# An MLP in two stages of seven-product recursion: source order on four engines, single passes from twelve to twenty

## The chip, the cores and the metric

The kernel runs on one core of one Trainium2 chip. Times are device microseconds (us) of one execution; the time of a kernel is the median of several executions. PE is the matrix engine (TensorE), DVE the vector engine, ACT the scalar engine, POOL the GpSimd engine, and SP the engine from whose queue all transfers of this kernel's MLP are issued. PSUM is the memory that PE writes products to.

## The reference

One layer of an encoder, applied to 1024 and to 256 tokens (1280 in all, width 1024): a mixing stage with DeltaNet and attention heads, and then the MLP, which is all that this change touches.

```
x = x + rmsnorm(mix, norm_mix_post)
hm = rmsnorm(x, norm_mlp_pre)
f = square(relu(hm @ w_up)) @ w_down          # w_up: 1024 x 4096, w_down: 4096 x 1024, float32
y = x + rmsnorm(f, norm_mlp_post)
```

## The kernel before, in words

*Precision.* A float32 product is made of three fast products: each operand is split into a high part, made by a cast on ACT, and a low part, made by a subtraction on DVE or POOL (`split`, lines L79 and L80). PE then adds hi times hi, hi times lo and lo times hi.

*Recursion.* Both matrix products of the MLP are computed blockwise by a scheme that makes a product of 2 x 2 blocks from seven products instead of eight. For the up product the 2 x 2 blocks are of `w_up` (256 columns of it, one "pair", two blocks of 512 rows by two of 128 columns) and of the normalised tokens. The scheme needs four sums of weight blocks per pair (`up_sums`, tiles `us`, L1128 to L1131) and sums of token blocks, which `to_M` makes (L1039 to L1042). `prep_m(j, i)` splits token operand j of half i into `mh` and `ml`, 128 by 1280 each.

*Up stage.* The 1280 tokens form two halves. `PASSES` lists what is done: NF pairs with the first half alone ("single passes"), then the other pairs with both halves ("double passes"), then the first NF pairs with the second half alone. With NF = 6 that is 6 + 10 + 6 passes; there are 16 pairs. A pass has seven products (`UP`), and a product is 12 matmuls of 128 by 128 by 320 for each half (`up_mm`, L1145 to L1147). `up_w` makes the weights of one product ready: the cast on ACT (tile `uhi`) and the subtraction on DVE (tile `ulo`). `up_post` takes a product out of PSUM: product 0 by a copy on ACT (L1168), the others by an addition on DVE (L1171 to L1198, two for product 4); products 1, 4, 5 and 6 complete a block, which ACT passes through relu and square (L1154, L1155), and from products 5 and 6 POOL makes sums for the down stage (L1190 to L1192, L1201). SP stores the results to `r_d`.

*Order.* A planner, which has its own estimate of each instruction's time, puts every engine's instructions in order before the kernel runs; on the chip each engine then keeps to that list. The order of the source enters as a priority. In the loop over products `s`, weights are made two products ahead (`up_w(*seq[s + 2])`), in three places for `uhi` and three for `ulo`. The four sums of a pair stand together where its first weights are made, on DVE in single passes and on POOL in double ones. The second half's seven `prep_m` come every fourth product from s = 10. The last token tile's norm (`norm`) takes steps at s = 3 to 6, and `to_M` of the last three tiles comes at the start, at s = 1 and at s = 7.

*Down stage.* It reads the stored blocks back in 49 steps of seven products (`DN`), five row tiles each (`prod`, L1283 to L1285), and adds them into ten tiles `acc` in DVE (L1289, L1291). `down_load` loads and sums blocks of `w_down` on POOL (L1237 to L1242), `down_r` loads a row operand `fr`, `down_prep` splits both (L1265 to L1271). The first of these are placed inside the last single passes, at products counted by `k`. At the end the products of the first two pairs, done as plain blocks, go into `acc` tile by tile (L1452 to L1456), followed by `rest`: a multiplication with the norm's weights (L1422), the root of the mean square (L1425 to L1430), the final multiply-and-add (L1434) and the store.

Of the kernel before, what the change touches and what calls it, by code (L numbers as in the profile page):

```python
# [10 lines left out]
F32R = mybir.dt.float32r  # L11
# [3 lines left out]
ALU = mybir.AluOpType  # L15
# [46 lines left out]
def build(ctx, tc, I, O):  # L62
# [14 lines left out]
    def split(hi, lo, src, heng=None, leng=None):  # L77

        (S.copy if heng is None else heng)(hi, src)  # L79
        (V if leng is None else leng).tensor_tensor(lo, src, f32(hi), ALU.subtract)  # L80
# [912 lines left out]
    def run(g):  # L993
        try:
            while True:
                next(g)
        except StopIteration as e:
            return e.value
# [25 lines left out]
    def to_M(xn, t, eng=G):  # L1024
        g = []
        for i in range(2):
            tp = tr_tile("xt")
            for k in range(4):
                T.transpose(tp[:, k * 128:(k + 1) * 128], xn[:, (i * 4 + k) * 128:(i * 4 + k + 1) * 128], ident)
            g.append(tp.rearrange("p (k c) -> p k c", k=4))  # L1030
        for i, cs, ts in halves(t):
            g0, g1 = (x[:, :, ts] for x in g)
            if i == 0:
                for j, x in ((0, g0), (1, g1)):
                    S.copy(mc[j, t // HT][:, :, cs], x)
            else:
                b11, b21, b22, t4, t1, t2, t3 = (mc[j, t // HT][:, :, cs] for j in range(7))
                S.copy(b22, g1)
                V.tensor_tensor(t1, g0, b11, ALU.subtract)  # L1039
                V.tensor_tensor(t3, b22, g0, ALU.subtract)  # L1040
                eng.tensor_tensor(t2, b22, t1, ALU.subtract)
                eng.tensor_tensor(t4, t2, b21, ALU.subtract)  # L1042
# [3 lines left out]
    def prep_m(j, i, leng=None):  # L1046
        mh[j, i] = p_tile5(h_slot[j, i], name="mh", dt=F32R)
        ml[j, i] = p_tile5(mspare[0], name="ml", dt=F32R)
        split(mh[j, i], ml[j, i], mc[j, i], leng=leng)
        mtag[j, i], mspare[0] = mspare[0], m_slot[j, i]  # L1050


    NF = 6
    PASSES = [*((p, (0,)) for p in range(NF)), *((p, (0, 1)) for p in range(NF, NP)), *((p, (1,)) for p in range(NF))]
    raws = {}

# [64 lines left out]
    ua = {}  # L1121

    def up_sums(n):
        a11, a12, a21, a22 = (raws[n][:, k:k + 4, f:f + 128] for f in (0, 128) for k in (0, 4))
        s = [uw.tile([128, 4, 128], F32, tag=f"us{x}", name="us", bufs=1) for x in range(4)]
        ua[n] = [a11, a12, a22, *s]
        eng = V if PASSES[n][1] != (0, 1) else G
        eng.tensor_tensor(s[0], a21, a22, ALU.add)  # L1128
        eng.tensor_tensor(s[1], s[0], a11, ALU.subtract)
        eng.tensor_tensor(s[2], a11, a21, ALU.subtract)  # L1130
        eng.tensor_tensor(s[3], a12, s[1], ALU.subtract)  # L1131

    def up_w(n, i):

        if n not in ua:
            up_sums(n)
        hi = uw.tile([128, 4, 128], F32R, tag="uhi", name="uhi", bufs=3)
        lo = uw.tile([128, 4, 128], F32R, tag="ulo", name="ulo", bufs=3)
        split(hi, lo, ua[n][UP[i][0]])
        return hi, lo  # L1140

    def up_mm(w, b, i):
# [106 lines left out]
    def down_r(s):  # L1249
        fr[s] = ring("fr", s, (Q, HW))  # L1250
        SP.dma_start(out=fr[s], in_=r_src(s // 7, s))
# [9 lines left out]
    def down_prep(s):  # L1261

        n, i = divmod(s, 7)
        fo[s] = hi, lo = ring("fhi", s, (Q, HW), F32R), ring("flo", s, (Q, HW), F32R)
        S.copy(hi, fr[s])  # L1265
        if i % 2:
            G.tensor_tensor(lo, fr[s], f32(hi), ALU.subtract)
        dw[s] = w_split(n, DN[i][1], ring("dhi", s, (Q, 512), F32R))
        yield
        if i % 2 == 0:  # L1270
            V.tensor_tensor(lo, fr[s], f32(hi), ALU.subtract)  # L1271
        del fr[s]
# [19 lines left out]
                seen_acc.add((t, d))  # L1292


    ws = {0: (w0[:, 0], w0[:, 1])}
    norm = out_norm(NT - 1, *prev)
    xlate = prev[2]
    to_M(*late[0], V)
    up_sums(0)
    ws[1] = up_w(*seq[1])  # L1300
    for s, (n, i) in enumerate(seq):
        p, parts = PASSES[n]
        if s == 1:
            to_M(*late[1], V)
        if s + 2 < len(seq):
            ws[s + 2] = up_w(*seq[s + 2])
        w = ws.pop(s)
        for h in parts:
            up_post(p, i, h, up_mm(w, UP[i][1], h))
        if i == 6 and n + 2 < len(PASSES):  # L1310
            up_raw(n + 2)
        if s == 0:
            for _, j in UP[NM:]:
                prep_m(j, 0)
        if 2 < s < 7:
            next(norm, None)
        elif s == 7:
            to_M(xlate, NT - 1, V)
            nstack.close()
            mr = ctx.enter_context(pool("mr"))  # L1320
            h_slot |= {(j, 1): place(mr, j) for j in range(7)}
        if s > 9 and (s - 10) % 4 == 0 and s < 38:
            j = UP[(s - 10) // 4][1]
            prep_m(j, 1)
        k = s - (len(seq) - 7 * NF)
        if k == 0:

            hm = [[(h_slot[j, h], mtag[j, h]) for _, j in UP] for h in range(2)]
            a, b = ([mspare[0]] + [x for y in hm[0] for x in y]), [x for y in hm[1] for x in y] + [w_slot]
            slots = {("w", 0): a[0:8], "fr": [a[8], a[9], b[0]], "fhi": [a[10], a[11], b[2]], "flo": [a[12], a[13], b[3]],  # L1330
                     "dhi": [a[14], b[1], b[4]], ("w", 1): b[5:13]}
            extra = b[13:15]
        if k in (4, 12, 18, 24):
            down_load(0, (4, 12, 18, 24).index(k))
        k -= 7 * NF - 21
        if k in (-3, 1, 15, 18):
            down_r((-3, 1, 15, 18).index(k))
        if k in (8, 13):
            run(down_prep((8, 13).index(k)))
    us.close()  # L1340
    ac = ctx.enter_context(pool("ac", side="right"))
    acc = [ac.tile([128, DM], F32, name=f"acc{t}") for t in range(NT)]
# [73 lines left out]
    def rest(c, h, ss):  # L1416

        t = c + h * HT
        last = (c, h) == (HT - 1, 1)
        r = ac.tile([128, 4], F32, tag="rsq", name="rsq", bufs=3)  # L1420
        for d in range(2):
            (V if last else G).tensor_tensor(half(t, d), half(t, d), wpf[:, d * 512:d * 512 + 512], ALU.mult)  # L1422
            if not last:
                yield
        V.tensor_tensor(r[:, 0:1], ss[:, 0:1], ss[:, 1:2], ALU.add)  # L1425
        S.activation(r[:, 1:2], r[:, 0:1], AF.Sqrt, scale=1.0 / DM, bias=eps)
        V.tensor_scalar(r[:, 2:3], r[:, 0:1], -0.5 / DM, -0.5 * EPS, ALU.mult, ALU.add)
        V.reciprocal(r[:, 1:2], r[:, 1:2])
        V.scalar_tensor_tensor(r[:, 3:4], r[:, 1:2], r[:, 2:3], r[:, 1:2], ALU.mult, ALU.mult)  # L1429
        V.scalar_tensor_tensor(r[:, 3:4], r[:, 3:4], 1.5, r[:, 1:2], ALU.add, ALU.mult)  # L1430
        yield
        for c0, n in ((0, 512), (512, 512)) if c == HT - 1 else ((0, DM),):
            cs = slice(c0, c0 + n)
            V.scalar_tensor_tensor(acc[t][:, cs], acc[t][:, cs], r[:, 3:4], x1s[c][:, h, cs], ALU.mult, ALU.add)  # L1434
            for ps_, t0, t1 in rows_of(c, h):
                SP.dma_start(out=y_out(t0, t1, cs), in_=acc[t][ps_, cs])
        if h and c + 2 < HT:
            x1s[c + 2] = x1_tiles(c + 2)
# [4 lines left out]
    for c in range(HT):  # L1443
        tk = slice(c * 128, c * 128 + 128)
        for h in range(2):
            ss = ac.tile([128, 2], F32, tag="ss", name="ss", bufs=3)
            for d in range(2):
                pm = p_tile()
                for m in range(2):
                    r, w = lrow[h, m], lwt[m, d]  # L1450
                    for k in range(Q):
                        T.matmul(pm, lhsT=r[0][:, k, tk], rhs=w[0][:, k], start=(m == k == 0), stop=False)  # L1452
                        T.matmul(pm, lhsT=r[0][:, k, tk], rhs=w[1][:, k], start=False, stop=False)
                        T.matmul(pm, lhsT=r[1][:, k, tk], rhs=w[0][:, k], start=False, stop=(m == k == 1))
                t = c + h * HT
                V.tensor_tensor(half(t, d), half(t, d), pm, ALU.add)  # L1456
                S.activation(junk, half(t, d), AF.Square, accum_out=ss[:, d:d + 1])  # L1457
                for _ in range(2):
                    if rests and next(rests[0], "end") == "end":
                        rests.pop(0)  # L1460
            rests.append(rest(c, h, ss))
            if h == 0 and c + 1 < HT:
                fix(c + 1)
# [31 lines left out]
```

## Time and profile before

| what | value |
|---|---|
| median of 3 runs | 1739.7 us (1735.0 to 1739.98) |
| the profiled execution's own time | 1741.06 us |
| its span, first to last instruction | 1739.3 us |
| PE busy | 1626.4 us, 94% |
| DVE busy | 1267.9 us, 73% |
| ACT busy | 854.6 us, 49% |
| POOL busy | 735.8 us, 42% |
| mean granted PE clock | 0.981 |
| up products | 905.6 to 1332.5 us of the span |
| down products | 1332.5 to 1727.8 us |

The profile's page gives busy time by engine and by group of instructions, with the idle time of the engine before each group and what ended it. A view by stretches gives the busy time of every engine between two moments, and the timeline lists instructions in order with the start, the duration, the line, the tile written and read, and in brackets the idle time before it and what ended that. An engine's busy share over the span hides stages with different limits, so the stretches are read stage by stage.

### The profile page before, as it was taken

What the parts mean: (1) busy time and instruction counts of PE and PEld (TensorE: products, weight loads), DVE (VectorE), ACT (ScalarE), POOL (GpSimd) and SP (SyncE); (2) the same over time, 40 slices, a digit from 0 to 9 for tenths busy, and PEclk for the clock granted to TensorE, in tenths of its full rate; (3) what the DMA queues carried; (4) which work ended last, traced back from release to release, by engine and by line L of the source; (5) the groups of instructions that cost most, each with busy time, mean ns of one, the idle gap of its engine ahead of it and who ended that gap; (6) DMA issues with size and microseconds to landing.
All of it is one profiled execution on the core that took longest, in us unless ns stands there. A gap on an engine that the chain in (4) does not pass through costs nothing. (4 is left out here: it accounts for less than half of the span.)

```text
span 1739.3 us, 27944 instructions
## 1 busy us (share of the span) xinstructions
PE 1626.4 (94%) x9799; PEld 1387.8 (80%) x9799; DVE 1267.9 (73%) x2549; ACT 854.6 (49%) x1937; POOL 735.8 (42%) x658
## 2 busy tenths in 40 slices
PE   6999898898997999889988999999989999999997
PEld 5777776777775888668878999999888888888885
DVE  7546798996744778885759954545787978888777
ACT  5236566554345767674446644544465333333422
POOL 3212231321113334440102555554636777788763
PEclk9999999999998999999999999999999999999999
DMA  6113334445447866244333543444556544444234
GB/s 208 70 42 109 97 108 129 137 133 154 133 143 231 273 203 194 79 161 166 104 127 127 178 147 125 151 135 134 187 193 220 154 140 146 132 143 142 86 115 155
DMA packets 208779, 252.68 MB, mean 145 GB/s; under 512 B 35073, under 2 KB 163391, under 8 KB 208639
## 3 DMA queue, kind: packets, MB, share of 16 engines
q1 hardware_dynamic: 208495, 250.77, 45.9%
q8 instruction: 77, 1.26, 0.3%
q14 instruction: 63, 0.52, 0.1%
q0 software_dynamic: 144, 0.13, 0.0%
HBM read 159.75 MB, written 91.10 MB: 144 GB/s over the span
## 5 line engine op out<-in xcount | busy, mean ns | idle before, releaser
L1146 PE MATMUL pd<-mh,ulo 128*128 128x320 f32 x892 | 279.6, 314 | 12.9 <-DVE ulo L80 12.8
L1145 PE MATMUL pd<-mh,uhi 128*128 128x320 f32 x892 | 276.6, 311 | 5.5 <-ACT uhi L79 5.5
L1147 PE MATMUL pd<-ml,uhi 128*128 128x320 f32 x892 | 276.9, 311 | 0.0
L1289 DVE TENSOR_TENSOR acc<-acc,pd 128x512 f32<-128x512 f32 x330 | 206.7, 678 | 44.1 <-PE pd L1285 44.1
L1283 PE MATMUL pd<-dhi,fhi 128*128 128x512 f32 x490 | 192.2, 392 | 1.0 <-DVE acc L1291 1.0
L1284 PE MATMUL pd<-dl,fhi 128*128 128x512 f32 x490 | 192.3, 393 | 0.0
L1285 PE MATMUL pd<-dhi,flo 128*128 128x512 f32 x490 | 191.9, 392 | 0.0
L1146 PEld LDWEIGHTS pd<-mh,ulo 128*128 128x128 f32 x892 | 169.1, 190 | 17.8 <-DVE ulo L80 17.8
L367 PE MATMUL pt<-h_hi,whi 128*128 128x512 f32 (+1 forms) x480 | 178.5, 372 | 0.0
L369 PE MATMUL pt<-h_hi,wlo 128*128 128x512 f32 (+1 forms) x480 | 178.4, 372 | 0.0
L368 PE MATMUL pt<-h_lo,whi 128*128 128x512 f32 (+1 forms) x480 | 178.4, 372 | 0.0
L1145 PEld LDWEIGHTS pd<-mh,uhi 128*128 128x128 f32 x892 | 168.9, 190 | 7.0 <-ACT uhi L79 7.0
L1147 PEld LDWEIGHTS pd<-ml,uhi 128*128 128x128 f32 x892 | 169.0, 190 | 0.0
L1265 ACT CAST fhi<-fr 128x1280 fp32r<-128x1280 f32 x49 | 62.1, 1267 | 212.6 <-PE pd L1284 116.2
L80 POOL TENSOR_TENSOR dl<-dw,dhi 128x1024 fp32r<-128x1024 f32 x49 | 129.0, 2633 | 43.4 <-ACT dhi L79 42.8
L1190 POOL TENSOR_TENSOR s<-u,u 128x320 f32<-128x320 f32 x32 | 34.3, 1071 | 207.6 <-ACT u L1155 140.7
L727 POOL TENSOR_TENSOR P<-P,sm 128x512 f32<-128x512 f32 (+1 forms) x72 | 73.5, 1040 | 95.3 <-DVE sm L725 39.0
L1283 PEld LDWEIGHTS pd<-dhi,fhi 128*128 128x128 f32 x490 | 92.0, 188 | 22.4 <-DVE acc L1291 1.4
L1285 PEld LDWEIGHTS pd<-dhi,flo 128*128 128x128 f32 x490 | 92.0, 188 | 20.7
L1284 PEld LDWEIGHTS pd<-dl,fhi 128*128 128x128 f32 x490 | 92.0, 188 | 20.3
L80 DVE TENSOR_TENSOR ulo<-us,uhi 128x512 fp32r<-128x512 f32 x88 | 76.3, 869 | 43.4 <-ACT uhi L79 42.5
L367 PEld LDWEIGHTS pt<-h_hi,whi 128*128 128x128 f32 x480 | 92.7, 193 | 13.5
(358 smaller groups left out, 4091.0 us busy)
## 6 DMA issues: line engine op xcount, KB each, us to landing
fr<-r_d SPq DMA_DIRECT2D x49, 640.0 KB, 4.3
vis<-vis_d SPq DMA_DIRECT2D x64, 384.0 KB, 4.2
uraw<-in_w_up SPq DMA_DIRECT2D x22, 1024.0 KB, 5.4
r_d<-s SPq DMA_DIRECT2D x128, 160.0 KB, 1.8
r_d<-u SPq DMA_DIRECT2D x96, 160.0 KB, 2.1
dw<-in_w_down SPq DMA_DIRECT2D x28, 512.0 KB, 4.9
wraw<-in_w_in SPq DMA_DIRECT2D x48, 256.0 KB, 3.7
x<-in_x_prompt SPq DMA_DIRECT2D x16, 512.0 KB, 3.4
```

Source lines behind the costliest of these rows:

```text
L80: (V if leng is None else leng).tensor_tensor(lo, src, f32(hi), ALU.subtract)
L367: T.matmul(pm[:, :n], lhsT=whi, rhs=h_hi[:, k, t0:t0 + n], start=(k == 0), stop=False)
L368: T.matmul(pm[:, :n], lhsT=whi, rhs=h_lo[:, k, t0:t0 + n], start=False, stop=False)
L369: T.matmul(pm[:, :n], lhsT=wlo, rhs=h_hi[:, k, t0:t0 + n], start=False, stop=(k == KD - 1))
L727: G.tensor_tensor(x[:, :kw], x[:, :kw], sm[:, 0:1].to_broadcast([128, kw]), ALU.mult)
L1145: T.matmul(pm, lhsT=w[0][:, k], rhs=mh[b, i][:, k], start=(k == 0), stop=False)
L1146: T.matmul(pm, lhsT=w[1][:, k], rhs=mh[b, i][:, k], start=False, stop=False)
L1147: T.matmul(pm, lhsT=w[0][:, k], rhs=ml[b, i][:, k], start=False, stop=(k == 3))
L1283: T.matmul(pm, lhsT=r[0][:, k, tk], rhs=w[0][:, k], start=(k == 0), stop=False)
L1284: T.matmul(pm, lhsT=r[0][:, k, tk], rhs=w[1][:, k], start=False, stop=False)
L1285: T.matmul(pm, lhsT=r[1][:, k, tk], rhs=w[0][:, k], start=False, stop=(k == Q - 1))
L1289: V.tensor_tensor(half(t, d), half(t, d), pm, ALU.add)
```

## The change

- From the start of the up products to the end, PE, DVE, ACT and POOL issue their instructions in the order in which the source emits them; the planner orders SP alone, as before.
- NF is 10: passes are 10 + 6 + 10.
- Weights are made three products ahead. High and low part lie in one tile, and there are four places for it: three of their own (`u1` to `u3`) and `w_slot`, which held the first product's weights.
- The four sums of a pair are no longer emitted together: two after the weights of its product 1, one after those of product 2, one after those of product 4.
- The second half's `prep_m` come one per pass, at s = 14, 21, ... 56. The norm's steps move to s = 4, 5, 7 and 8, the last `to_M` to s = 10.
- The down stage's first loads and splits are placed over the ten last single passes: `down_load` at k = 10, 30, 36, 42, `down_r` at 20, 24, 66, 67, `down_prep` at 60 and 65.
- In the tail the last tile's multiplication with the norm's weights follows each of its two additions at once, the other tile of the last pair is multiplied on DVE instead of POOL, and three steps of the tile before are emitted after each product instead of two.

```diff
-    NF = 6
+    NF = 10
...
         eng = V if PASSES[n][1] != (0, 1) else G
+        yield
         eng.tensor_tensor(s[0], a21, a22, ALU.add)
         eng.tensor_tensor(s[1], s[0], a11, ALU.subtract)
+        yield
         eng.tensor_tensor(s[2], a11, a21, ALU.subtract)
+        yield
         eng.tensor_tensor(s[3], a12, s[1], ALU.subtract)
...
-        if n not in ua:
-            up_sums(n)
-        hi = uw.tile([128, 4, 128], F32R, tag="uhi", name="uhi", bufs=3)
-        lo = uw.tile([128, 4, 128], F32R, tag="ulo", name="ulo", bufs=3)
+        if n not in sums:
+            sums[n] = up_sums(n)
+            next(sums[n])
+        x = (7 * n + i) % 4
+        hl = (uw.tile([128, 2, 4, 128], F32R, tag=f"u{x}", name="uhl", bufs=1) if x else
+              p_tile5(w_slot, (2, 4, 128), "uhl", F32R))
+        hi, lo = hl[:, 0], hl[:, 1]
         split(hi, lo, ua[n][UP[i][0]])
+        if i in (1, 2, 4):
+            next(sums[n], None)
...
+    ctx.enter_context(tc.manual_schedule(engines={getattr(mybir.EngineType, x) for x in ("PE", "DVE", "Activation", "Pool")}))
...
+    ws[1] = up_w(*seq[1])
     to_M(*late[0], V)
-    up_sums(0)
-    ws[1] = up_w(*seq[1])
+    M1 = dict(zip(range(14, 14 + 7 * 7, 7), UP))
     for s, (n, i) in enumerate(seq):
         p, parts = PASSES[n]
-        if s == 1:
+        if s == 2:
             to_M(*late[1], V)
-        if s + 2 < len(seq):
-            ws[s + 2] = up_w(*seq[s + 2])
+        for x in (2, 3) if s == 0 else (s + 3,):
+            if x < len(seq):
+                ws[x] = up_w(*seq[x])
         w = ws.pop(s)
         for h in parts:
             up_post(p, i, h, up_mm(w, UP[i][1], h))
...
-        if s > 9 and (s - 10) % 4 == 0 and s < 38:
-            j = UP[(s - 10) // 4][1]
-            prep_m(j, 1)
+        if s in M1:
+            prep_m(M1[s][1], 1)
...
-        for d in range(2):
-            (V if last else G).tensor_tensor(half(t, d), half(t, d), wpf[:, d * 512:d * 512 + 512], ALU.mult)
-            if not last:
-                yield
+        for d in () if last else range(2):
+            (V if c == HT - 1 else G).tensor_tensor(half(t, d), half(t, d), wpf[:, d * 512:d * 512 + 512], ALU.mult)
+            yield
...
-                for _ in range(2):
+                if (c, h) == (HT - 1, 1):
+                    V.tensor_tensor(half(t, d), half(t, d), wpf[:, d * 512:d * 512 + 512], ALU.mult)
+                for _ in range(2 if c < HT - 1 else 3):
```

More of the change, by code (lines that the diff above doesn't have):

```diff
@@ L1127, in up_sums @@
         eng = V if PASSES[n][1] != (0, 1) else G
+        yield
         eng.tensor_tensor(s[0], a21, a22, ALU.add)
         eng.tensor_tensor(s[1], s[0], a11, ALU.subtract)
+        yield
         eng.tensor_tensor(s[2], a11, a21, ALU.subtract)
+        yield
         eng.tensor_tensor(s[3], a12, s[1], ALU.subtract)
+    sums = {}
     def up_w(n, i):
-        if n not in ua:
-            up_sums(n)
-        hi = uw.tile([128, 4, 128], F32R, tag="uhi", name="uhi", bufs=3)
-        lo = uw.tile([128, 4, 128], F32R, tag="ulo", name="ulo", bufs=3)
+        if n not in sums:
[5 more added lines that the diff above has]
+        hi, lo = hl[:, 0], hl[:, 1]
         split(hi, lo, ua[n][UP[i][0]])
+        if i in (1, 2, 4):
+            next(sums[n], None)
         return hi, lo
@@ L1311, in build @@
             up_raw(n + 2)
-        if s == 0:
+        if s == 1:
             for _, j in UP[NM:]:
                 prep_m(j, 0)
-        if 2 < s < 7:
+        if s in (4, 5, 7, 8):
             next(norm, None)
-        elif s == 7:
+        elif s == 10:
             to_M(xlate, NT - 1, V)
@@ L1332, in build @@
             extra = b[13:15]
[L1333 to L1339, printed above, removed]
+        if k in (10, 30, 36, 42):
+            down_load(0, (10, 30, 36, 42).index(k))
+        if k in (20, 24, 66, 67):
+            down_r((20, 24, 66, 67).index(k))
+        if k in (60, 65):
+            run(down_prep((60, 65).index(k)))
     us.close()
```

## The prediction

> **What bounds the kernel now.** I read the page first: TensorE (PE) is busy 94% of the span, and its lines L1145 to L1147 are the first products of the MLP. The idle time in front of them is small on the page, so I went on to busy time by stretch.
>
> ```profile
> span 1739.3 us, 27944 instructions
> PE 1626.4 (94%) x9799; PEld 1387.8 (80%) x9799; DVE 1267.9 (73%) x2549; ACT 854.6 (49%) x1937; POOL 735.8 (42%) x658
> L1146 PE MATMUL pd<-mh,ulo 128*128 128x320 f32 x892 | 279.6, 314 | 12.9 <-DVE ulo L80 12.8
> ```
>
> In the next view the stretches run from the last VectorE (DVE) operation of one pass, L1198, to that of the next; columns are length, then busy us of PE, weight loads, DVE, ACT, POOL, then the granted clock. The last two rows are the up products as a whole and the down products.
>
> ```profile
> 905.60:945.50 39.90, 32.41 (x199) 29.67 (x198) 37.72 (x67) 27.13 (x50) 4.76 (x4) 0.96 0.40 132
> 945.50:959.70 14.20, 13.09 (x87) 12.41 (x86) 14.20 (x22) 9.54 (x20) 6.17 (x4) 1.00 0.51 166
> 974.10:986.60 12.50, 11.84 (x77) 11.32 (x78) 12.50 (x21) 6.81 (x15) 3.33 (x3) 1.00 0.47 153
> 1022.80:1047.40 24.60, 24.60 (x170) 24.60 (x170) 12.18 (x21) 12.24 (x25) 12.77 (x13) 1.00 0.42 137
> 1246.10:1266.80 20.70, 12.89 (x77) 11.40 (x76) 15.77 (x19) 9.79 (x19) 12.39 (x9) 0.93 0.62 208
> 1305.40:1318.00 12.60, 12.60 (x88) 12.60 (x87) 11.32 (x19) 7.67 (x17) 4.21 (x4) 1.00 0.56 183
> 905.60:1332.50 426.90, 406.46 (x2707) 399.46 (x2706) 294.26 (x459) 234.66 (x465) 206.03 (x173) 0.99 0.48 158
> 1332.50:1727.80 395.30, 394.25 (x1712) 320.83 (x1711) 314.32 (x451) 127.80 (x149) 292.42 (x126) 1.00 0.44 138
> ```
>
> A pass with both halves (168 matmuls) takes 24.6 us with PE never idle, 0.146 us a matmul; so a product of 12 matmuls is 1.76 us and a single pass 12.3 us at best. All 2688 up matmuls need 394 us; the stretch is 427, so some 30 us (with 3 us of transposes) are what better ordering could win. They lie in the first four passes and at 1246 to 1267. The down products have 1 us of idle. Single passes are tight elsewhere: DVE is busy 11.3 of 12.6 us.
>
> **The change, part by part.** *Order.* From the up products on, four engines issue in source order. Per product s the source says: cast the weights of s+3 to hi (ACT), subtract to lo (DVE), perhaps weight sums (DVE), multiply (PE), then the post step of s: a DVE add from PSUM and, in products 1, 4, 5 and 6 of a pass, relu and square on ACT. ACT thus has cast(s+4) behind the relu pair of s, which waits for DVE's add of s; DVE has split(s+4) before its add of s+1. That closes a ring: add, relu, square, cast, split, next add. Before, the order was another: at 1316.78 the add of product 5 is followed by a split whose cast had already run, then the add of product 6, and only then the split whose cast follows the relu pair.
>
> ```profile
> 1309.28 1.25 DVE L1130 TENSOR_TENSOR us<-uraw 128x512 f32<-128x512 f32 x1
> 1315.78 0.48 DVE L1182 TENSOR_TENSOR u<-u,pd 128x320 f32<-128x320 f32 x1
> 1316.17 0.68 DVE L80 TENSOR_TENSOR ulo<-uraw,uhi 128x512 fp32r<-128x512 f32 x1
> 1316.78 0.48 DVE L1186 TENSOR_TENSOR u<-u,pd 128x320 f32<-128x320 f32 x1
> 1317.41 0.69 DVE L80 TENSOR_TENSOR ulo<-uraw,uhi 128x512 fp32r<-128x512 f32 x1 [0.15 <-ACT uhi L79]
> 1318.02 0.48 DVE L1198 TENSOR_TENSOR u<-u,pd 128x320 f32<-128x320 f32 x1
> 1318.81 0.96 DVE L80 TENSOR_TENSOR ulo<-us,uhi 128x512 fp32r<-128x512 f32 x1 [0.31 <-ACT uhi L79]
> ...
> 1306.91 0.41 ACT L1168 COPY u<-pd 128x320 f32<-128x320 f32 x1
> 1307.21 0.62 ACT L79 CAST uhi<-us 128x512 fp32r<-128x512 f32 x1
> 1317.29 0.47 ACT L1154 ACTIVATE u<-u 128x320 f32<-128x320 f32 x1
> 1318.17 0.60 ACT L79 CAST uhi<-us 128x512 fp32r<-128x512 f32 x1
> ...
> 1318.34 0.88 POOL L1190 TENSOR_TENSOR s<-u,u 128x320 f32<-128x320 f32 x1 [8.36 <-ACT u L1155]
> ```
>
> From the add (1316.78) over relu (1317.29), square and cast (1318.17) to the split (1318.81) is 2.03 us; the split holds DVE 0.60 (1316.17 to 1316.78): 2.63 us to the next add, where PE takes 1.76. An add alone holds DVE 0.40 (1315.78 to 1316.17), a sum, of the split's form, 0.60. One single pass in source order, counted from the start of its add 1, with PE never in the way:
>
> - add 2 at 2.63 (one ring); adds 3 and 4, with no relu between, each after an add and a split: 3.63 and 4.63;
> - add 5 after a ring and two sums, 8.46; add 6 after a ring and one sum, 11.69;
> - then, product 0 having no add: relu pair 1.39, cast 0.60, PSUM copy 0.30 (1306.91 to 1307.21), cast 0.60, split 0.60, sum 0.60: the next pass's add 1 at 15.78.
>
> Of the 15.8 us DVE waits over 6, in turn with ACT. POOL's sums of products 5 and 6 come on top, since they and DVE hold each other up where both read SBUF: beside POOL's 1318.34 the split at 1318.81 took 0.96 instead of 0.69, the sum at 1309.28 took 1.25. Three or four such operations a pass make some 1.2 us. I take 17.0, between 15.8 (no blocking) and 18 (twice that), because these rows are the same operations in the same neighbourhood.
>
> No row shows this order run, so the ring is my step from the code and the rows. That a queue is not overtaken, this trace shows: a cast of the down stage waits 5.09 us for its DMA, the weight cast behind it waits too, and PE with it.
>
> ```profile
> 1261.13 1.26 ACT L1265 CAST fhi<-fr 128x1280 fp32r<-128x1280 f32 x1 [5.09 <-DMA fr<-r_d]
> 1262.30 0.61 ACT L79 CAST uhi<-uraw 128x512 fp32r<-128x512 f32 x1
> ...
> 1262.96 0.41 PE L1145 MATMUL pd<-mh,uhi 128*128 128x320 f32 x1 [2.11 <-ACT uhi L79]
> 1265.96 0.63 PE L1146 MATMUL pd<-mh,ulo 128*128 128x320 f32 x1 [2.59 <-DVE ulo L80]
> ```
>
> [...]
>
> *Three ahead, four places.* One product more of slack, 1.76 us once; a ring that is longer than PE's pace uses any fixed slack up in its first pass.
>
> *Ten pairs alone.* Single passes go from 12 to 20, double ones from 10 to 6. PE's work stays; 28 more casts and splits, sums of eight more passes on DVE, four more loads of 1 MB. The stretch at 1305.40 carries such loads and stores at 183 GB/s with PE never idle, so the loads stay hidden; at PE's pace the rest would too; behind the ring each single pass costs 17.0 − 12.3 = 4.7 us. Double passes give the ring 3.5 us per product and put the sums on POOL: 24.6 stays.
>
> *Token halves prepared one per pass.* Before, two in a pass cost 1.9 us (14.20), one 0.2 (12.50). In source order its cast stands on ACT before the weight cast of product 1, and its subtraction on DVE before that split:
>
> ```profile
> 944.77 1.26 ACT L79 CAST mh<-mc 128x1280 fp32r<-128x1280 f32 x1
> 971.44 1.48 DVE L80 TENSOR_TENSOR ml<-mc,mh 128x1280 fp32r<-128x1280 f32 x1
> ...
> 924.65 1.27 DVE L1009 SCALAR_TENSOR_TENSOR x<-mix,rsq,x 128x1024 f32<-128x1024 f32 x1
> 925.96 1.06 ACT L1011 ACTIVATE mix<-x 128x1024 f32<-128x1024 f32 x1 [0.18 <-DVE x L1009]
> ...
> 1231.60 2.39 POOL L1237 TENSOR_TENSOR dw<-dw 128x1024 f32<-128x1024 f32 x1 [7.88 <-DMA dw<-in_w_down]
> 1231.72 2.82 DVE L1131 TENSOR_TENSOR us<-uraw,us 128x512 f32<-128x512 f32 x1
> ```
>
> The first two rows are its cast and subtraction. In the walk the last step becomes 1.39 + 0.60 + 0.30 + 1.26 + 1.48 + 0.60 + 0.60 = 6.23 for 4.09 (the weight cast now runs beside the subtraction): +2.1, so passes 2 to 8 take 19.1.
>
> *First two passes.* Two walks up to the last add (17.0 + 12.8), plus the seventh half 2.1, two tiles of token sums 2.4 each, the norm of the last tile 3.9 (1.27 and 1.06 in series, the rest small): 40.6 after the first add at 905.6 + 3.5, so 949.7 where it was 945.5.
>
> *Down stage's preparation.* Its DMAs are moved 40 products ahead of their casts, so the 5.09 us wait goes, and 8 us of the 20.70 us pass with it. In exchange four POOL sums of 1024 block a split each (between 0 and the 2.1 us of the last row, 2.82 for 0.69; I take 1.8 a piece, 7 us), and two preparations put a cast of 1.26 and a shorter one each into ACT's queue ahead of a weight cast, with a long DVE or POOL subtraction behind: 4 to 5 us each, 9 us. SP's queue stays the scheduler's; the stores wait on data they waited on before.
>
> *Tail.* The last tile's adds stood behind the tile before:
>
> ```profile
> 1727.35 0.40 PE L1454 MATMUL pd<-lwt,lrow 128*128 128x512 f32 x1
> 1729.39 0.68 DVE L1456 TENSOR_TENSOR acc<-acc,pd 128x512 f32<-128x512 f32 x1
> 1730.92 0.69 DVE L1422 TENSOR_TENSOR acc<-acc,wpf 128x512 f32<-128x512 f32 x1 [0.19 <-ACT junk L1457]
> 1733.66 0.15 DVE L1425 TENSOR_TENSOR rsq<-ss 128x1 f32<-128x1 f32 x1
> 1734.83 0.75 DVE L1434 SCALAR_TENSOR_TENSOR acc<-acc,rsq,x 128x512 f32<-128x512 f32 x1
> ```
>
> The last matmul ends at 1727.75, and 12 matmuls of 0.23 earlier the first of the tile's two products did, 1725.0, but its add came at 1729.39. Now it comes at 1725.0; multiply at 1726.5 (the 1.53 of the rows), the other tile's two multiplies and root chain (1.17) to 1729.5; second add, multiply to 1731.6; two final steps 1.4, root chain, to 1734.2 instead of 1734.83: −0.6 (−2 to +1). The down loop keeps its order in kind: 0 ± 3, less its 1 us of idle.
>
> *Sum.* Last add of pass 1 949.7; passes 2 to 8, 133.5; pass 9, 17.0: 1100.2. PE runs ahead of that add: in the walk the weights of product 5 are split by 2.63 and those of product 6 by 3.63, so the two products can end at 2.63 + 2 × 1.76 = 6.15, and product 6 is added at 12.8: PE is through 6.7 earlier, 1093.5. Six double passes 147.6: 1241.1. Second group: first add +3.5, first walk +0.65, nine walks 153, to add 6 12.8, preparation 16, less 6.7: 1420.4, where the up products ended at 1332.5. So +88, −1, −0.6: span 1825.6. The profiled execution took 1741.06 around its span of 1739.3 and lies 1.4 above the median of 1739.7: forecast 1826.
>
> **The rivals.** *PE stays the bound (faster).* If casts and splits keep ahead, the 30 us shrink to about 5 (one half per pass costs 0.2; no DMA wait): 1739.7 − 27 = 1713. For it speaks that single passes ran in 12.6 with the same work. It decides where the ring is under 12.3 us a pass; the rows give 15.8 without any blocking. *Half clock.* If the stalls (up to 2.6 us in the walk) keep the clock low, products become PE's own bound:
>
> ```profile
> 913.21 0.47 PE L1145 MATMUL pd<-mh,uhi 128*128 128x320 f32 x1
> 913.48 0.47 PE L1146 MATMUL pd<-mh,ulo 128*128 128x320 f32 x1
> ```
>
> 0.27 a matmul, 22.4 a pass: 20 × 22.4 + 147.6 for 427, 1909. Against it: the stretch with gaps of 2.11 and 2.59 still had a mean of 0.93. *Nothing moves:* the scheduler had this order in substance; the rows above show otherwise. 1740.
>
> **How the numbers follow.** Ring 0.80; PE stays the bound 0.12; half clock 0.04; nothing 0.04. The ring's own range: without blocking 17.0 becomes 15.8 and the preparation 8: 1795; with 18 a pass and 2 us per double pass: 1858. Ordering the trace may soften further (fewer sums on the ring) reaches 1760. Range 1758 to 1862. A 0.3% change, 5 us, is what a measurement here can tell: faster 0.12, same 0.04, slower 0.84.
>
> **What would show it.** Right: single passes at 16 to 18 us, DVE waiting on ACT's cast and ACT on DVE's add in turn, PE idle before splits, double passes at 24.6, the 5.09 us DMA wait gone. Wrong: single passes near 12.5 with no such alternation.

## The result, and the profile after

The changed kernel takes 1839.8 us (median of 4 executions, 1837.5 to 1842.1) against 1739.8 us for the kernel before, in executions on the same chip: a ratio of 1.0576, 95% interval 1.0544 to 1.0607. It is slower by 100 us; the forecast was 1826 us with a range of 1758 to 1862.

First the page of the changed kernel: its head, and the groups whose idle time has grown. The last columns of a group are busy us and mean ns, then the idle time before its instructions and what ended most of it.

```profile
span 1835.7 us, 28081 instructions
PE 1661.0 (90%) x9799; PEld 1402.9 (76%) x9799; DVE 1307.8 (71%) x2611; ACT 861.9 (47%) x1965; POOL 709.4 (39%) x640
L1155 PE MATMUL pd<-mh,uhl 128*128 128x320 f32 x892 | 288.5, 323 | 42.0 <-ACT uhl L79 41.7
L1156 PE MATMUL pd<-mh,uhl 128*128 128x320 f32 x892 | 291.5, 327 | 35.4 <-DVE uhl L80 35.2
L80 DVE TENSOR_TENSOR uhl<-us,uhl 128x512 fp32r<-128x512 f32 x104 | 96.5, 936 | 138.9 <-ACT uhl L79 138.9
L1164 ACT ACTIVATE u<-u 128x320 f32<-128x320 f32 x128 | 60.1, 469 | 239.4 <-DVE u L1191 62.4
```

Of the kernel before, the first and the third of these groups:

```profile
L1145 PE MATMUL pd<-mh,uhi 128*128 128x320 f32 x892 | 276.6, 311 | 5.5 <-ACT uhi L79 5.5
L80 DVE TENSOR_TENSOR ulo<-us,uhi 128x512 fp32r<-128x512 f32 x88 | 76.3, 869 | 43.4 <-ACT uhi L79 42.5
```

PE waited 5.5 us for ACT's casts and 12.9 for DVE's low parts before; now it waits 42.0 and 35.4. DVE in turn has waited 138.9 us for ACT's casts in this one group, where it was 43.4, and ACT's relu 239.4 us, most often for an add of DVE. No engine is fuller than 90%, and three wait for one another.

Busy time by stretch, changed kernel, columns as in the prediction: the first two passes, a single pass of the first group with a token half to prepare, a double pass, two single passes of the second group (one plain, one with two preparing sums of the down stage on POOL), then the up and the down products as a whole.

```profile
903.00:952.30 49.30, 35.78 (x218) 32.63 (x217) 37.12 (x66) 21.61 (x46) 6.51 (x7) 0.97 0.36 115
952.30:971.20 18.90, 14.22 (x86) 12.49 (x85) 12.60 (x20) 8.85 (x17) 4.22 (x5) 1.00 0.36 117
1149.60:1174.20 24.60, 24.60 (x169) 24.60 (x169) 12.07 (x21) 11.79 (x25) 13.18 (x13) 1.00 0.41 136
1264.70:1281.70 17.00, 14.66 (x87) 13.91 (x86) 11.12 (x20) 7.68 (x16) 4.24 (x5) 0.90 0.42 140
1315.60:1337.00 21.40, 16.75 (x87) 15.16 (x86) 15.53 (x19) 7.67 (x16) 9.76 (x7) 0.84 0.31 103
903.00:1426.70 523.70, 444.60 (x2706) 417.14 (x2705) 328.63 (x518) 240.75 (x491) 178.99 (x155) 0.96 0.42 136
1426.70:1821.60 394.90, 394.90 (x1711) 321.49 (x1710) 315.59 (x448) 128.63 (x150) 294.50 (x125) 1.00 0.43 138
```

The up stage went from 426.9 to 523.7 us (+96.8), the down stage from 395.3 to 394.9, what follows the last matmul from 11.5 to 14.1 (+2.6), and the up stage starts 2.6 earlier: 96.4 in all, the difference of the spans. A double pass is 24.6 as before. A plain single pass is 17.0 where the kernel before had 12.5, and in it DVE, busiest but PE, is busy only 11.1 us.

The timeline of the changed kernel, in one plain single pass; the bracket is the idle time before an instruction.

```profile
1302.87 0.47 DVE L1181 TENSOR_TENSOR u<-u,pd 128x320 f32<-128x320 f32 x1
1304.89 0.69 DVE L80 TENSOR_TENSOR uhl<-us,uhl 128x512 fp32r<-128x512 f32 x1 [1.55 <-ACT uhl L79]
1305.49 0.48 DVE L1185 TENSOR_TENSOR u<-u,pd 128x320 f32<-128x320 f32 x1
...
1313.49 0.96 DVE L80 TENSOR_TENSOR uhl<-us,uhl 128x512 fp32r<-128x512 f32 x1 [1.55 <-ACT uhl L79]
1314.37 1.35 DVE L1132 TENSOR_TENSOR us<-uraw 128x512 f32<-128x512 f32 x1
1315.64 0.47 DVE L1208 TENSOR_TENSOR u<-u,pd 128x320 f32<-128x320 f32 x1
...
1303.37 0.47 ACT L1164 ACTIVATE u<-u 128x320 f32<-128x320 f32 x1 [1.82 <-DVE u L1181]
1303.87 0.47 ACT L1165 ACTIVATE u<-u 128x320 f32<-128x320 f32 x1
1304.25 0.60 ACT L79 CAST uhl<-us 128x512 fp32r<-128x512 f32 x1
...
1315.13 1.32 POOL L1202 TENSOR_TENSOR s<-u,u 128x320 f32<-128x320 f32 x1
```

Read it from add to add: add of product 1 at 1302.87, its relu at 1303.37, the square at 1303.87, the cast of product 5's weights at 1304.25, the subtraction for it at 1304.89 after 1.55 us in which DVE had nothing else that it was allowed to do, and the add of product 2 at 1305.49. That add stood in the queue behind the subtraction and did not pass it, though its product had long been there: PE's last matmul ahead of product 4 began at 1299.10. From add to add it is 2.62 us. Beside POOL's sums the subtraction takes 0.96 and the weight sum 1.35 instead of 0.69.

### The profile page after: what moved, and what is told of

Its sections match the earlier page's. It is cut to its first block, busy times and chain, and to the rows that moved or that the text cites. A ratio compares the mean times of both kernels' runs of the same rounds, so it can differ in the third digit from the quotient of the medians.

```text
span 1835.7 us, 28081 instructions
## 1 busy us (share of the span) xinstructions
PE 1661.0 (90%) x9799; PEld 1402.9 (76%) x9799; DVE 1307.8 (71%) x2611; ACT 861.9 (47%) x1965; POOL 709.4 (39%) x640
## 5 line engine op out<-in xcount | busy, mean ns | idle before, releaser
L1155 PE MATMUL pd<-mh,uhl 128*128 128x320 f32 x892 | 288.5, 323 | 42.0 <-ACT uhl L79 41.7
L1156 PE MATMUL pd<-mh,uhl 128*128 128x320 f32 x892 | 291.5, 327 | 35.4 <-DVE uhl L80 35.2
L1157 PE MATMUL pd<-ml,uhl 128*128 128x320 f32 x892 | 283.8, 318 | 0.0
L1155 PEld LDWEIGHTS pd<-mh,uhl 128*128 128x128 f32 x892 | 174.8, 196 | 53.9 <-ACT uhl L79 53.8
L1156 PEld LDWEIGHTS pd<-mh,uhl 128*128 128x128 f32 x892 | 175.0, 196 | 50.7 <-DVE uhl L80 50.7
L80 DVE TENSOR_TENSOR uhl<-us,uhl 128x512 fp32r<-128x512 f32 x104 | 96.5, 936 | 138.9 <-ACT uhl L79 138.9
L1157 PEld LDWEIGHTS pd<-ml,uhl 128*128 128x128 f32 x892 | 175.5, 197 | 0.0
L1164 ACT ACTIVATE u<-u 128x320 f32<-128x320 f32 x128 | 60.1, 469 | 239.4 <-DVE u L1191 62.4
L1200 POOL TENSOR_TENSOR s<-u,u 128x320 f32<-128x320 f32 x32 | 28.9, 904 | 352.4 <-ACT u L1165 352.4
L80 POOL TENSOR_TENSOR dl<-dw,dhi 128x1024 fp32r<-128x1024 f32 x49 | 134.0, 2735 | 33.3 <-ACT dhi L79 33.3
```

Of the source, the lines that this page charges most:

```text
L1155: T.matmul(pm, lhsT=w[0][:, k], rhs=mh[b, i][:, k], start=(k == 0), stop=False)
L1156: T.matmul(pm, lhsT=w[1][:, k], rhs=mh[b, i][:, k], start=False, stop=False)
L1157: T.matmul(pm, lhsT=w[0][:, k], rhs=ml[b, i][:, k], start=False, stop=(k == 3))
```

## The experiments

Four theories are put to the test: *the ring* (adds of DVE wait behind subtractions that wait for casts that wait behind relus of earlier adds), against *the passes* (more single passes, places and moved steps cost, whatever the order), *POOL* (its sums that hold DVE up are the main cause) and *the lead* (how many products the weights are ahead).

**The order taken away.** From the changed kernel one line goes.

```diff
-    ctx.enter_context(tc.manual_schedule(engines={getattr(mybir.EngineType, x) for x in ("PE", "DVE", "Activation", "Pool")}))
```

> The changed kernel without the line that puts the four engines into the order of the source; ten pairs of single passes, four weight places, three products ahead, the moved steps and the new tail all stay. Ring theory (ACT's cast stands behind relu and square of an earlier product, DVE's add of the next product behind the subtraction that waits for this cast): the planner can put cast and subtraction elsewhere, the ring is not there, single passes come back to about the time of TensorE's products, 12.3 to 13 us instead of 17.0, so 20 x 4 to 4.7 us go: 1740 to 1760 us, at the lowest 1713. Rival (the number of single passes, the places or the moved steps cost the time, whatever the order): within 15 us of 1840.

Measured: 1739.3 us, ratio to the kernel before 1.0008 (0.9997 to 1.0019). A plain single pass of this kernel by stretch:

```profile
1250.50:1262.90 12.40, 12.40 (x86) 12.40 (x86) 11.74 (x19) 7.71 (x17) 4.66 (x4) 1.00 0.55 175
```

PE is busy for all of its 12.4 us. Twenty single passes, four places, three products ahead and the moved steps together cost nothing under the planner, which may also place the moved steps elsewhere; the 100 us need the order. The passes as a cause by themselves are out.

**The order alone.** The same line is added to the kernel before, and nothing else.

> The kernel before with only the line that puts the four engines into the order of the source; six pairs of single passes, three weight buffers, two products ahead, the old tail. Ring theory: the same ring closes, since cast and subtraction of product s+2 are issued ahead of the add of product s; some 3.3 to 4.4 us for each of the 12 single passes are 40 to 53 us, with a few more where a preparation or a late transfer stands in the queue: 1780 to 1800 us. Rival (order is harmless, the further single passes or places cost): 1735 to 1745 us.

Measured: 1785.7 us, ratio 1.0284 (1.0258 to 1.0309). By stretch, the shortest single pass of its second group and a double one:

```profile
1284.40:1299.80 15.40, 13.61 (x84) 12.37 (x84) 10.42 (x19) 7.81 (x16) 3.77 (x5) 1.00 0.47 154
1119.20:1143.30 24.10, 24.10 (x166) 24.10 (x165) 11.96 (x20) 11.90 (x25) 12.77 (x13) 1.00 0.41 139
```

The ring closes in the old kernel too, and only single passes pay (the double row runs from the second of a pass's two last adds to the first of the next pass's, hence 24.1). Here the pass is 15.4 and not 17.0; it also has the four sums together, and only two products' lead, so the difference is not one of the order alone.

**Eight pairs alone instead of ten.**

```diff
-    NF = 10
+    NF = 8
...
-    M1 = dict(zip(range(14, 14 + 7 * 7, 7), UP))
+    M1 = dict(zip(range(14, 14 + 6 * 7, 6), UP))
```

(The down stage's first steps move to k = 6, 20, 25, 30; 14, 18, 52, 53; 46, 51.)

> The changed kernel with eight pairs of single passes instead of ten, eight double passes instead of six; the steps tied to products are moved along. Ring theory: two singles at 17.0 us each give way to one double at 24.6 us, twice: 2 x (34.0 - 24.6) = 19 us less, 1815 to 1825 us. Rival (the time lies in the first passes, in the moved steps and the tail, not in every single pass): within 5 us of 1840.

Measured: 1814.8 us, 25 below the changed kernel; of the two traces' spans (24.0 apart) the up stage holds 22.5. The time scales with the number of single passes. It moved 3.7 us more than the two exchanged pairs give; the token halves' other places are in it, and this was not taken apart.

**The ring opened.** The kernel stays in the order of the source; only DVE's subtraction and the sums are issued behind the post step.

```diff
-        split(hi, lo, ua[n][UP[i][0]])
-        if i in (1, 2, 4):
-            next(sums[n], None)
+        src = ua[n][UP[i][0]]
+        S.copy(hi, src)
+
+        def second():
+            V.tensor_tensor(lo, src, f32(hi), ALU.subtract)
+            if i in (1, 2, 4):
+                next(sums[n], None)
+
+        if 7 * n + i < 4:
+            second()
+        else:
+            later.append(second)
...
             up_post(p, i, h, up_mm(w, UP[i][1], h))
+        while later:
+            later.pop(0)()
```

> The changed kernel, still in the order of the source on all four engines, with one move: the cast of the weight tile of product s+3 stays ahead of product s, but DVE's subtraction for it and the sums of the next tiles are issued behind the adds of product s. Ring theory: the way add, relu, square, cast, subtraction, add now spans two products (2.6 us against 3.5 us of products), so TensorE sets the pace again: single passes 12.3 to 13 us, 20 x 4 to 4.7 us less, 1745 to 1760 us. [...]

Measured: 1772.5 us, ratio 1.0207 (1.0181 to 1.0234): 67 us of the 100 are gone with that one move, 12 to 27 fewer than the ring theory said. A plain single pass by stretch is

```profile
1245.80:1259.20 13.40, 12.97 (x86) 12.36 (x86) 11.86 (x20) 7.94 (x16) 4.16 (x5) 1.00 0.53 173
```

and the 1.0 us that it is still above PE's 12.4 shows in the timeline of the same kernel, at the turn of the pass:

```profile
1257.28 0.68 DVE L1129 TENSOR_TENSOR us<-uraw 128x512 f32<-128x512 f32 x1
1258.00 1.25 DVE L1130 TENSOR_TENSOR us<-us,uraw 128x512 f32<-128x512 f32 x1
1259.18 0.47 DVE L1218 TENSOR_TENSOR u<-u,pd 128x320 f32<-128x320 f32 x1
1260.00 1.38 DVE L1152 TENSOR_TENSOR uhl<-us,uhl 128x512 fp32r<-128x512 f32 x1 [0.35 <-ACT uhl L1149]
```

Sum, cast and subtraction of the next pass's weights follow one another exactly while POOL makes its sums, and DVE's instructions take up to twice their time (1.25 and 1.38 us, where the sum ahead of them takes 0.68). The eight passes with a token half take 15.7 us here, 3.3 above PE's pace, so they hold more of what is left than the plain ones.

**POOL's sums left out.** In the changed kernel, products 5 and 6 store tiles that exist in place of the sums.

```diff
-            s = r["s"] = [u_tile(f"s{x}") for x in range(4)]
             a11, a21, a22 = r[1], r["u"], r[4]
-            G.tensor_tensor(s[0], a21, a22, ALU.add)
-            G.tensor_tensor(s[1], s[0], a11, ALU.subtract)
-            G.tensor_tensor(s[2], a11, a21, ALU.subtract)
-            for x in range(3):
-                out(3 + x, s[x])
+            for x, y in enumerate((a11, a21, a22)):
+                out(3 + x, y)
...
-            s = r["s"]
-            G.tensor_tensor(s[3], s[1], r[3], ALU.subtract)
             out(1, r[3])
-            out(6, s[3])
+            out(6, r[3])
```

> The changed kernel without POOL's four sums s in the up stage; the tiles that are already there are stored in their place, so as many bytes go out, and four of the seven stored arrays hold other values. Ring theory with the prediction's blocking term (about 1.2 us in each single pass, since DVE's instructions get long beside POOL's): single passes 15.8 instead of 17.0 us, 20 x 1.2 = 24 us less, 1810 to 1820 us. If POOL only filled idle time: within 5 us of 1840. If POOL and not the ring were the main cause, single passes would come to 13 us or less and the time to 1760 or less.

Measured: 1808.2 us, 32 below the changed kernel. By stretch, a plain single pass:

```profile
1283.70:1299.70 16.00, 13.70 (x86) 12.50 (x86) 10.01 (x20) 7.69 (x16) 0.00 (x0) 1.00 0.43 138
```

With POOL idle the pass is 15.9 from last add to last add (the edges of the row are rounded), 1.05 less: the ring without blocking that the prediction's walk put at 15.8. So POOL adds to the ring, and is not the cause. Twenty times 1.05 us (16.98 against 15.93) are 21; some 9 of the other 11 lie in three passes of the second group in which POOL also sums for the down stage: 15.9 us here, like the plain ones, where the changed kernel took 21.4, 19.2 and 19.2. Here POOL, with none of its own four sums of a pass ahead of them in its list, makes those sums at 1217.6 to 1228.5, beside the last double pass.

**The square left out.** One ACT instruction less in each result; the output is that of relu.

```diff
         S.activation(x, x, AF.Relu)
-        S.activation(x, x, AF.Square)
```

> The changed kernel without the square behind the relu (the output is that of relu alone): one ACT instruction less, about 0.50 us from its start to the next start, in each of the four results of a pass and half. Ring theory: all four stand in the ring of a single pass, 4 x 0.50 = 2.0 us less for each, 20 x 2.0 = 40 us, 1795 to 1805 us, the double passes unchanged at 24.6. Rival (ACT is busy 47% and never sets the time): within 5 us of 1840.

Measured: 1796.5 us, 43 below the changed kernel. Stretch of a plain single pass, 14.98 from add to add:

```profile
1254.80:1269.70 14.90, 13.88 (x91) 13.13 (x90) 11.02 (x19) 5.81 (x12) 4.14 (x5) 1.00 0.46 147
```

ACT, busy 47% of the span, gives back 2.0 us of a 17.0 us pass for four instructions of 0.5: each stands in the way that sets the end. This dose is the strictest test of the ring, and it came out at the size.

**Two products ahead.**

```diff
-        for x in (2, 3) if s == 0 else (s + 3,):
+        for x in (s + 2,):
```

> The changed kernel with weights made two products ahead instead of three, still in four places. Ring theory: the ring goes from add through relu, square, the next cast and its subtraction to the next add, however many products the cast is ahead; single passes stay at 17.0 us, 1835 to 1845 us. Rival (a cast that waits for its place, which the product just before frees, holds ACT and sets 17 us): a place is free one product earlier, and the time falls by 20 us or more. Third (the lead over TensorE is what is short): slower by 10 us or more.

Measured: 1866.7 us, 27 above the changed kernel, so the expectation failed. The timeline of this kernel, and the length of the plain pass that ends at 1294.2:

```profile
1306.90 0.69 DVE L80 TENSOR_TENSOR uhl<-uraw,uhl 128x512 fp32r<-128x512 f32 x1 [1.16 <-ACT uhl L79]
1307.51 0.48 DVE L1196 TENSOR_TENSOR u<-u,pd 128x320 f32<-128x320 f32 x1
1309.54 0.95 DVE L80 TENSOR_TENSOR uhl<-uraw,uhl 128x512 fp32r<-128x512 f32 x1 [1.55 <-ACT uhl L79]
1310.41 1.35 DVE L1129 TENSOR_TENSOR us<-uraw 128x512 f32<-128x512 f32 x1
1311.80 1.25 DVE L1130 TENSOR_TENSOR us<-us,uraw 128x512 f32<-128x512 f32 x1
1312.97 0.47 DVE L1208 TENSOR_TENSOR u<-u,pd 128x320 f32<-128x320 f32 x1
```

```profile
1275.50:1294.20 18.70, 14.53 (x84) 12.46 (x84) 11.78 (x19) 7.89 (x16) 4.21 (x4) 1.00 0.38 126
```

The ring is there with the same 1.55 us wait, but the two sums now stand one add later, in the turn from product 5 to 6, where POOL works: 5.46 us from add to add where the changed kernel has 4.18. Nothing here showed whether the lead mattered besides, so the sums were moved back with two products' lead kept.

```diff
-        if i in (1, 2, 4):
+        if i in ((0, 1, 3) if n else (1, 2, 4)):
```

> Two products ahead as in the run that came out 27 us slower than the changed kernel, but with the sums of a pass issued one product earlier, so that they stand between the same adds as with three ahead. Placement theory (with two ahead the sums s0 and s1 fell one add later, beside POOL's sums, and took 1.35 and 1.25 us instead of 0.69; the ring itself was the same 2.65): single passes back to 17.0 us, 1835 to 1848 us. Lead theory (two products of lead are too few): single passes stay at 18.75 and the time within 6 us of 1867.

Measured: 1845.7 us. The plain pass and the two sums:

```profile
1288.40:1305.40 17.00, 13.61 (x86) 12.37 (x85) 11.12 (x19) 7.69 (x16) 4.17 (x5) 1.00 0.40 130
```

```profile
1299.94 0.69 DVE L1129 TENSOR_TENSOR us<-uraw 128x512 f32<-128x512 f32 x1
1300.66 0.69 DVE L1130 TENSOR_TENSOR us<-us,uraw 128x512 f32<-128x512 f32 x1
```

The plain pass is at 17.0 again with two products' lead. The lead itself is worth at most the 8 us by which this up stage (531.6) is longer than the changed kernel's, outside the plain passes.

**Sums early, the ring open.** The opened kernel, with the sums issued after the weights of products 0, 1 and 4.

```diff
-            if i in (1, 2, 4):
+            if i in ((0, 1, 4) if n else (1, 2, 4)):
```

> The kernel with the subtractions behind the adds, and besides the first three sums of a pass are issued one product earlier on DVE, ahead of POOL's sums. If what is left above 12.3 us in its single passes (13.41) is the chain sum, cast, subtraction at the turn of the pass, with DVE instructions at twice their length beside POOL's, 0.6 to 1.1 us of it goes: 1750 to 1762 us. If DVE is simply full, the pass stays at 13.4 and the time within 4 us of 1772.

Measured: 1742.3 us, ratio 1.0029 (1.0012 to 1.0046), 30 below the opened kernel, better than expected. By stretch, a pass with a token half and a plain one:

```profile
1013.50:1027.40 13.90, 12.90 (x86) 12.37 (x85) 12.77 (x21) 8.98 (x18) 4.23 (x5) 1.00 0.50 160
1225.40:1237.70 12.30, 12.30 (x86) 12.30 (x85) 11.10 (x19) 7.81 (x17) 4.22 (x4) 1.00 0.59 195
```

The plain pass is at PE's pace, in source order, with the changed kernel's passes, places and lead. The ring and the place of the sums together hold all of the change's 100 us but about 5.

**Towards a version below both.** From that kernel: the subtraction of a prepared token half one product behind its cast, the old tail, and the order of the source ended (`om.close()`) with the up stage.

```diff
...
+            S.copy(mh[j, i], mc[j, i])
+            behind.append(lambda: V.tensor_tensor(ml[j, i], mc[j, i], f32(mh[j, i]), ALU.subtract))
...
+        while behind:
+            behind.pop(0)()
...
+    om.close()
     us.close()
```

> The kernel with subtractions behind the adds and sums early, and three moves more: DVE's subtraction of each prepared mixed tile is issued one product behind its cast (0.79 us of DVE's wait for ACT goes in each of seven passes, if the pass follows DVE), the order of the source ends with the up stage, and the tail is that of the kernel before. Expected from 1742: about 5.5 us for the seven waits, 2.6 us for the tail (14.1 to 11.5), 1730 to 1737 us, so slightly below the kernel before; if DVE is bound by its work and not by the wait, 1738 to 1741, no difference.

Measured: 1739.4 us, ratio 1.0009 (0.9995 to 1.0023), above the 1730 to 1737 expected. The passes with a token half went from 13.98 to 13.15, by 0.83 as expected, the tail from 14.1 to 12.8 only; but the last single pass took 15.1 instead of 12.5 and the down stage 397.0 instead of 393.9. The last run moved the end of the order to the start of the last tiles.

> The last version with the end of the source order moved from the end of the up stage to the start of the last tiles, so that the six recursive down passes keep it too. If the 2.6 us that its last single pass lost (15.1 against 12.5) and its down stage of 397.0 us came from the planner's choice at that boundary, they go back to 12.5 and 393.9 us, as in the runs with the order throughout: 1733 to 1737 us, 3 to 5 below the last version. If the boundary has nothing to do with it: 1737 to 1741.

Measured: 1735.6 us, ratio 0.9985 (0.9971 to 0.9998). Its two stages:

```profile
897.00:1321.80 424.80, 406.07 (x2708) 399.30 (x2707) 317.64 (x518) 244.07 (x491) 185.62 (x155) 0.99 0.51 165
1321.80:1715.70 393.90, 393.90 (x1712) 320.80 (x1710) 313.29 (x449) 129.63 (x150) 295.04 (x127) 1.00 0.45 142
```

The last pass is back at 12.5 and the down stage has no idle time on PE: the planner's choice at the boundary had cost that. The version lies 104 us below the changed kernel and 3 us below the kernel before. The 3 us are under the 0.3% that counts as a difference here, and the version's up stage, 424.8, is still 31 above the 394 of PE's matmuls.

## Why the prediction was right, and where its steps were off

*The order and the ring: right.* Predicted 2.63 us from add to add, found 2.62. That it is the cause is shown from four sides: no order, no loss; the order alone brings a loss; one of the two queued steps moved, and two thirds of the loss go; an instruction taken out of the ring shortens each pass by its length times four. The other signs came too: double passes at 24.6, and in the up stage no cast of the down stage waits for its DMA any more, where one had waited 5.09 us.

*The single pass: right.* 17.0 predicted, 17.0 found; without POOL 15.8 and 15.9, so the blocking term of 1.2 was 1.0. With a token half 19.1 against 18.9. The timeline of the changed kernel shows the blocking on both engines: beside POOL the sum of two SBUF tiles at 1314.37 took 1.35 us for 0.69, while the add at 1315.64, which takes one input from PSUM, kept its 0.47 in the middle of POOL's 1.32; and POOL's sums at 1313.98 and 1315.13, beside that sum, took 1.20 and 1.32, where the one at 1313.03 took 0.87. What makes each slow the other down is not shown.

*The sum* gave 514.8 us of up products; 523.7 were found. Part by part, at the prediction's own marks (last adds as far as pass 9, PE's matmuls from there on):

| part | predicted | found | |
|---|---|---|---|
| passes 0 and 1 | 44.1 | 49.3 | token sums, the norm and the ring together cost 5.2 more than the list of terms; which of them was not taken apart |
| passes 2 to 9 | 150.5 | 147.6 | pass 9 took 14.8, not 17.0: the next pass is double, its sums are POOL's, and none stands in DVE's ring |
| double passes, to PE's last matmul of them | 140.9 | 144.0 | PE's run ahead of 6.7 was mis-sized: PE was through 3.8 before the last add of pass 9, at 1096.2 |
| second group, to the first down product | 179.3 | 182.7 | add 1 of its first pass came 7.9 after PE's last matmul of the double passes, not 3.5 + 0.65 |

The preparation inside the second group came to about 16 as predicted, but its two parts were off in opposite ways, so that is luck: a preparing sum on POOL cost 2.2 us and not 1.8 (4.4, 2.2 and 2.2 over the plain pass), and the two preparations of operands 4.2 and 2.9, not 9 together. The 2.9 are in the last pass, where PE's last matmul ends 9.3 after add 1; in the plain pass that ends at 1392.3 it ends 6.4 after it. With the tail, which follows, and an up stage that starts 2.6 earlier, the span came out 10 us above the sum.

*Three ahead: the step was wrong.* The prediction gave the third product of lead "one product more of slack, 1.76 us once". Against two ahead it is worth 27 us here, 21 of them not as lead, since they went when the sums alone were moved back: the lead decides between which adds the sums fall.

*The tail: the wrong sign.* Predicted −0.6, found +2.6. The failing step is "Now it comes at 1725.0", that the last tile's first add comes when its product ends. The timeline of the changed kernel in the tail, DVE and PE's last matmul:

```profile
1817.98 0.68 DVE L1465 TENSOR_TENSOR acc<-acc,pd 128x512 f32<-128x512 f32 x1
1819.69 0.16 DVE L1437 RECIPROCAL rsq<-rsq 128x1 f32<-128x1 f32 x1 [0.78 <-ACT rsq L1435]
1820.23 0.68 DVE L1465 TENSOR_TENSOR acc<-acc,pd 128x512 f32<-128x512 f32 x1
1820.83 1.28 DVE L1443 SCALAR_TENSOR_TENSOR acc<-acc,rsq,x 128x1024 f32<-128x1024 f32 x1
1822.02 0.68 DVE L1465 TENSOR_TENSOR acc<-acc,pd 128x512 f32<-128x512 f32 x1
1826.40 0.68 DVE L1465 TENSOR_TENSOR acc<-acc,pd 128x512 f32<-128x512 f32 x1
...
1821.22 0.40 PE L1463 MATMUL pd<-lwt,lrow 128*128 128x512 f32 x1
```

The last tile's products end at about 1818.9 (twelve matmuls of 0.23 before the last) and 1821.6; their adds come at 1822.0 and 1826.4, since DVE still has the tile before in its queue, whose root chain waits 0.78 for ACT's root behind ACT's squares. From the end of the last matmul to the end of the span, the traces give:

| | old tail | new tail |
|---|---|---|
| planner | 11.5 (kernel before) | 12.3 (order taken away) |
| source order | 13.1 (order alone) | 14.1 (changed kernel) |

By these four the source order costs 1.6 to 1.8 us there and the reordered tail 0.8 to 1.0. But the last two versions, with the old tail and the planner there, took 12.8 and 12.7 where the kernel before took 11.5, so how the 2.6 us divide between order and tail is not shown closer than about 1.3.

## What to carry to other kernels

When engines are put into the order of the source, write each engine's list down and look for a way round: a step of the next products queued ahead of one that completes this product, on two engines in turn, set the pace here by its latency (2.62 us from add to add, where PE takes 1.76 for a product), though no engine was full. Issue what finishes a product before what waits for a helper's next result, so that the way round spans two products (67 of the 100 us here), and keep DVE's weight sums away from POOL's turn, where they took 1.35 and 1.25 us for 0.69. A lead of one more product was not only slack; it changed which instructions stand beside which, 21 of its 27 us.

## What the runs showed of the hardware

The granted clock of PE fell to half for 3.3 us in plain single passes of the changed kernel whose longest gap on PE is 1.35 us; in a plain pass with eight pairs alone, whose longest gap is 1.34, it did not, and both take 17.0 us. The stretch of the half clock inside the plain pass shown above (mean clock 0.90), and PE's first gap in that pass on the timeline:

```profile
1268.40:1271.70 3.30, 3.30 (x14) 3.30 (x14) 1.76 (x4) 2.26 (x5) 0.00 (x0) 0.50 0.18 64
```

```profile
1266.79 0.41 PE L1155 MATMUL pd<-mh,uhl 128*128 128x320 f32 x1 [1.35 <-ACT uhl L79]
```

Of the kernel with eight pairs alone:

```profile
1278.20:1295.20 17.00, 13.67 (x87) 12.43 (x86) 11.11 (x20) 7.69 (x16) 4.22 (x5) 1.00 0.42 140
```

So the half clock, a rival of the prediction, was met and cost nothing where the ring sets the pace; the changed kernel's own pass from 1375.3 to 1392.3 kept the full clock and took 17.0 too. What brought the clock down is not shown: PE's longest idle time is 1.35 us in the pass with the half clock and in the one without.
